# adaLN columns queued behind given units of weights, and gates written out and read back some units apart

## The chip, the cores and the metric

The kernel runs on one core of one Trainium2 chip. The metric is device time in microseconds (us) of one execution; lower is better. The engines are TensorE (PE, matmuls; PEld is its weight load), VectorE (DVE), ScalarE (ACT), GpSimd (POOL) and SyncE (SP), which here issues nearly all DMA transfers in one in-order queue (SPq).

## The reference

Two layers of a transformer-like backbone on 256 latent and 256 context tokens, model width 1024. Layer 0 mixes tokens by bidirectional retention (4 heads), layer 1 by neighbourhood attention (16 heads); each mixer is followed by a SwiGLU with hidden width 2816. Everything is modulated (adaLN): from the conditioning vectors `c` (latent) and `c_ctx` (context) come six rows per layer, a shift, a scale and a gate for each of the two sub-layers. Cut to what matters:

```
cond_lat = silu(c)[:, None, :]; cond_ctx = silu(c_ctx)[None, None, :]
for i in range(2):
    want_ctx = i < 1
    m_lat = split(cond_lat @ ada_w[i] + ada_b[i], 6)      # shift, scale, gate, shift, scale, gate
    m_ctx = split(cond_ctx @ ada_w[i] + ada_b[i], 6)
    a_lat = h_lat * (1 + m_lat[1]) + m_lat[0]             # and a_ctx alike
    y_ctx, y_lat = retention_mixer(...) if i == 0 else neighbourhood_mixer(...)
    h_lat = layer_norm(ALPHA * h_lat + m_lat[2] * y_lat, ln_g[i, 0], ln_b[i, 0])
    f_lat = swiglu(h_lat * (1 + m_lat[4]) + m_lat[3], ffn_w13[i], ffn_w2[i])
    h_lat = layer_norm(ALPHA * h_lat + m_lat[5] * f_lat, ln_g[i, 1], ln_b[i, 1])
    # the same for h_ctx while want_ctx
return h_lat
```

## The kernel before

**Matmuls and the stream of weights.** A matmul in fp32 is made of three in fp32r (`mm3`, L139 to L143): each operand is split into a high part (the value rounded to fp32r) and a low part (the rest), and the products high·high, low·high and high·low are summed in PSUM. All weight matrices pass once through SBUF as 228 "units" of 128 x 1024 fp32 (512 KB). The class `Stream` (L83 to L135) does that in three steps: `load_to` issues the load of `raw{u}` on SP (L110, three buffers); `split_to` has ACT cast the high part `whi{u}` (L123) and DVE subtract to get the low part `wlo{u}` (L125; a few on POOL), five buffers each; `next()` hands a unit to the matmuls after it has split units ahead (`ahead` = 4) and issued loads three further. Most units feed 24 matmuls of 512 columns.

**The order of the work.** Most of the program is ordered by a scheduler that simulates the engines' timelines and may issue a ready instruction earlier than where the code stands; some stretches are ordered as written (`manual_schedule`). Within an engine, and in SP's queue, instructions run in the order they are issued, each waiting for its own semaphores, so one that waits holds up all behind it.

**The adaLN columns.** The class `Ada` (L193 to L248) computes `silu(c) @ ada_w + ada_b` not on PE but on DVE: one "job" is 128 output columns, whose weights are loaded as `adaraw{i}` (128 x 1024 fp32, 512 KB, L218, two buffers), and one DVE instruction `junk{i}_{s}` (L226) multiplies them by the broadcast condition and sums along the row into one column of `ada{l}{s}`; s = 0 is latent, s = 1 context. There are 96 jobs. Jobs 0 to 15 (layer 0, shift and scale of the mixer) run at the start. Then come for layer 0 the mixer's gate (16 to 23), scale (24 to 31) and shift (32 to 39) of the SwiGLU, and its gate (40 to 47); for layer 1 scale and shift of the mixer (48 to 63), then, latent only and so one instruction each, its gate (64 to 71), scale (72 to 79), shift (80 to 87) and gate of the SwiGLU (88 to 95). `pump()` is called once per unit handed out and runs jobs by a credit per unit (`RATES`, 0.5, 0.7 or 1.0 by the number of jobs done), but the scheduler may move the instructions forward. `hooks` are functions called when a given number of jobs is done.

**Gates.** A gate is needed as a row on all partitions. `load_gate` (L266) stores the eight gate columns to DRAM (`gscr`, 128 x 8, 4 KB, L269) and reads the row back broadcast to 128 partitions as `gateb` (512 KB, L271). The two DMAs are issued one after the other on SP, and the second waits for the first to land. The gates of layer 0 are made by a hook at 24 jobs (mixer) and inside the first SwiGLU (`mix0`, `gate_hook`, at its fourth hidden block); those of layer 1 inside the attention (j = 2) and in the last SwiGLU. `make_affine` (L707) combines layer norm weights with scale and shift in three tiny POOL operations.

**Where they are used.** The retention's output projection `out_half` gives four PSUM tiles `w` of 512 columns; `head_add` (L591) has DVE multiply each by the gate into `t2` (two buffers) and POOL (or DVE) add it to `z`. In the SwiGLU, `hidden` makes the tiles `f` and DVE multiplies them with the SiLU part into `hf` (L813); `d` is the second matmul. `qf1k` (L457 on DVE, L462 its cast) is the rotary evacuation of the keys of head 1.

Of the kernel before, what the change touches and what calls it, by code (L numbers as in the profile page):

```python
# [8 lines left out]
F32 = mybir.dt.float32  # L9
# [3 lines left out]
ALU = mybir.AluOpType  # L13
# [5 lines left out]
P = 128  # L19
D = 1024  # L20
# [24 lines left out]
def backbone(ctx: ExitStack, tc: tile.TileContext, wpack, adapack, cond, condcol, xT, xtok, adab, lncol, lnrow,  # L45
             decay, delta, rope, rpb, mask8, out):
    nc = tc.nc
# [8 lines left out]
    act = ctx.enter_context(tc.tile_pool(name="act", **HIGH))  # L56
# [26 lines left out]
    class Stream:  # L83
# [21 lines left out]
        def load_to(self, n):  # L105
            n = min(n, self.total)
            while self.loaded < n:
                i = self.loaded
                t = wst.tile([P, UNIT], F32, tag="raw", name=f"raw{i}", bufs=3)
                nc.sync.dma_start(t, wpack[i])  # L110
                self.raw[i] = t
                self.loaded += 1

        def split_to(self, n):
            n = min(n, self.total)
            while self.split < n:
                u = self.split
                self.load_to(u + 1)
                raw = self.raw.pop(u)
                pool, th, tl, bufs = self.place.get(u, (wsplit, "whi", "wlo", self.BUFS))  # L120
                hi = pool.tile([P, UNIT], F32R, tag=th, name=f"whi{u}", bufs=bufs)
                lo = pool.tile([P, UNIT], F32R, tag=tl, name=f"wlo{u}", bufs=bufs)
                nc.scalar.copy(hi, raw)  # L123
                eng = nc.gpsimd if u in self.on_pool else nc.vector
                eng.tensor_tensor(out=lo, in0=raw, in1=hi.bitcast(F32), op=ALU.subtract)  # L125
                self.units[u] = (hi, lo)
                self.split += 1

        def next(self):
            self.split_to(self.used + self.ahead)  # L130
            self.load_to(self.split + 3)
            u = self.used
            self.used += 1
            ada.pump()
            return self.units.pop(u)  # L135

    stream = Stream()
# [17 lines left out]
    l0 = l0stack.enter_context(tc.tile_pool(name="l0", **HIGH))  # L155
# [37 lines left out]
    class Ada:  # L193
# [43 lines left out]
                    self.hooks.pop(self.done)()  # L237


        RATES = ((48, 0.5), (64, 0.7), (96, 1.0))  # L240

        def pump(self):
            if self.done < 16:
                return
            self.credit += next((r for n, r in self.RATES if self.done < n), 1.0)
            while self.credit >= 1:
                self.credit -= 1
                self.run(self.done + 1)  # L248

    ada = Ada()  # L250

# [11 lines left out]
    gscr = dram.tile([2, 2, 2, D], F32, name="gscr")  # L263
    gateb = {}

    def load_gate(l, g, s):  # L266

        scr = gscr[l, g, s]
        nc.sync.dma_start(scr.rearrange("(k p) -> p k", p=P), adacol[l][s][:, 8 * (3 * g + 2):8 * (3 * g + 2) + 8])  # L269
        t = (act, l0)[s].tile([P, D], F32, tag=f"gate{s}", name=f"gateb{l}{g}{s}")  # L270
        nc.sync.dma_start(t, scr.unsqueeze(0).partition_broadcast(P))  # L271
        gateb[(l, g, s)] = t

    lnrows = {}

# [28 lines left out]
    with Phase("ret", "yTh", "yTl", "vh", "vl", "kh", "kl") as rp:  # L304
# [466 lines left out]
        for t in CTX_FIRST:  # L771
            for half in range(2):
# [1 line left out]
                xr = rp.tile([P, 512], F32, tag="pf", name=f"xr{t}{half}", bufs=2)  # L774
                nc.sync.dma_start(xr, xtok[t, :, cs])
                nc.gpsimd.tensor_scalar(out=z[t][:, cs], in0=xr, scalar1=ALPHA, scalar2=0.0, op0=ALU.mult, op1=ALU.add)
        ada.hooks[24] = lambda: [load_gate(0, 0, s) for s in range(2)]
        ada.hooks[40] = lambda: [make_affine(0, 0, 0, 1, s) for s in range(2)]
        for h in range(RET_H):
            scores(h)  # L780
# [19 lines left out]
    with Phase("ffn", "hh", "hl") as fp:  # L800
# [23 lines left out]
        def mix0(part):  # L824

            js = list(range(HF))
            if part == 0:
                u0 = units(2)
                hidden(0, 0, u0, 256, 256, hcols(0, 256, 256))
                Feed(fam_of(fp), 0, 0, (0, 1)).all()  # L830
                u1 = units(2)
                hidden(0, 1, u1, 256, 256, hcols(1, 256, 256))
                region.__exit__(None, None, None)
                hidden(0, 0, u0, 0, 256, hcols(0, 0, 256))
                hidden(0, 1, u1, 0, 256, hcols(1, 0, 256))
                load_ln(fp, ("ln0", "ln1", "ln2", "ln3"), 0, 0)
                for t in CTX_FIRST:
                    residual(0, 0, t)
                js = js[2:]
            for j in js:  # L840
                hidden(0, HF * part + j, units(2), 0, 512, hid[j])
                if (part, j) == (0, 3):
                    for s in range(2):
                        gate_hook(0, 1, s)

            cur = {}

            def piece(half, k):
                n = half * HF + k
                if n // 2 not in cur:  # L850
                    cur[n // 2] = stream.next()
                return cut(cur[n // 2], slice(None), slice((n % 2) * 512, (n % 2) * 512 + 512))

            for half in range(2):
                cs = slice(half * 512, half * 512 + 512)
                ps = {t: bank(f"d{part}_{half}_{t}") for t in CTX_FIRST}
                tail = 7 if (part, half) == (1, 1) else 1
                groups = [[k] for k in range(HF - tail)] + [list(range(HF - tail, HF))]
                for grp in groups:
                    ms = [piece(half, k) for k in grp]  # L860

                    def products(t, n0=0, n1=len(grp)):
                        for k, m in list(zip(grp, ms))[n0:n1]:
                            mm3(ps[t], cut(hid[k], slice(None), slice(t * P, t * P + P)), m, k == 0, k == HF - 1)

                    if (part, half) == (1, 1) and grp[-1] == HF - 1:
                        return last_rows(products, ps)
                    for t in CTX_FIRST:
                        products(t)
                        if grp[-1] == HF - 1:  # L870
                            gate_add(0, 1, t, cs, ps[t], nc.vector if part else nc.gpsimd)
# [33 lines left out]
            normalise(1, *mr)  # L905
            return region

        def gate_hook(l, g, s):
            load_gate(l, g, s)

        mix0(0)
        ada.run(64)
        for s in range(2):
            make_affine(0, 1, 1, 0, s)
        T3, E3, E4, BB, FB, E5 = 2, 2, 7, range(7), 4, 2
        region = mix0(1)
        ada.run(96)
    l0stack.close()


    with Phase("na", "oTh", "oTl", "qs") as ap:
# [164 lines left out]
        for j in range(KT - 2):  # L1086
            load_bias(j + 2)
            kq(j + 2)
            na_transposes(j)
            if j == KT - 3:  # L1090
                region.__exit__(None, None, None)
                region = tc.manual_schedule(engines={PE, DVE, POOL, ACT})
                region.__enter__()
            na_scores(j + 1)
            na_products(j)
            if j < KT - 3:
                make_bias(j + 2)
            if j == 2:
                load_gate(1, 0, 0)
                make_affine(1, 0, 1, 1, 0)  # L1100


# [56 lines left out]
    with Phase("ffn1", "h1h", "h1l") as fp:  # L1159
# [51 lines left out]
                if RX:  # L1211
                    region.__exit__(None, None, None)

        load_gate(1, 1, 0)
        load_ln(fp, ("ln0", "ln1", "ln2", "ln3"), 1, 0)
        with tc.issue_after(last_pool.ins):
            for t in range(2):
# [154 lines left out]
```

## Time and profile before

| | us |
|---|---|
| median of 3 timed runs (lowest, highest) | 1241.11 (1240.41, 1245.79) |
| the profiled execution | 1235.01 |
| its span | 1233.2 |
| DVE, low parts `wlo` L125, 217 instructions | 287.2 busy |
| DVE, columns `junk` L226, 160 instructions | 215.0 busy, 81.1 idle just before them |
| landing of a unit's load `raw`, median | 4.1 |
| mean TensorE clock granted, of full speed | 0.981 |

A profile row of instructions names the source line, the engine, the operation and the tiles as output<-inputs, with the numbers in the names left out. In rows of waits the waiting line comes first, then the instruction that released it, then microseconds in total, number of times and the longest. A timeline row has start, duration, instruction and, in brackets, how long the engine had been idle before it and what ended that.

### The profile page before, as it was taken

Reading aid. Unit: us, or ns where it says so; the run is one execution under the profiler, and the core shown is the slowest. Engines: PE = TensorE matmul, PEld = TensorE weight load, DVE = VectorE, ACT = ScalarE, POOL = GpSimd, SP = SyncE. Lnnn points to the kernel's source line nnn. Section 1 sums busy time; section 2 is a strip of 40 time slices with the busy share of each in tenths; the row PEclk is TensorE's granted clock in tenths of the full one; section 3 lists DMA queues with packets and bytes.
Section 4 is the critical chain, followed back from the end, with each engine's and each line's share of the span. In section 5 each row is a group of like instructions: output and inputs, shape, how many; then the busy total and the mean of one; then the engine's idle time right before and its main releaser. Section 6 shows DMA issues by size and latency. Waiting matters only on the chain.

```text
span 1233.2 us, 15925 instructions
## 1 busy us (share of the span) xinstructions
PE 1172.8 (95%) x5990; PEld 985.8 (80%) x5990; DVE 769.5 (62%) x1079; ACT 441.0 (36%) x670; POOL 316.4 (26%) x304
## 2 busy tenths in 40 slices
PE   7989898999999999899879999999999998999996
PEld 5668686888888888688668788887888876999985
DVE  7898599833543589399567633247455576766544
ACT  3553231422333243122111333215354464555430
POOL 1521114412211568000002200006535446300003
PEclk9989999999999999999979999999999999999998
DMA  9855666523223223567988523324478744777550
GB/s 357 304 196 144 160 215 197 164 78 94 99 69 103 70 95 95 108 232 241 204 273 267 153 90 103 97 74 141 137 210 216 232 133 132 233 220 230 183 160 35
DMA packets 70156, 201.76 MB, mean 164 GB/s; under 512 B 14528, under 2 KB 17344, under 8 KB 70080
## 3 DMA queue, kind: packets, MB, share of 16 engines
q1 hardware_dynamic: 69648, 200.10, 53.4%
q8 instruction: 47, 0.77, 0.3%
q10 hardware_dynamic: 432, 0.66, 0.1%
q14 instruction: 29, 0.24, 0.1%
HBM read 187.98 MB, written 2.25 MB: 154 GB/s over the span
## 4 chain that ended last, share of the span: by engine, by line
PE 45%; DMA 7%; DVE 6%; issue 2%; POOL 1%; ACT 0%; SPq 0%; POOLq 0%; DVEq 0%; ACTq 0%
PE f L143 6%; PE f L142 6%; PE f L141 6%; DMA adaraw<-in_adapack 5%; PE d L142 2%; PE d L143 2%; PE d L141 2%; DVE junk L226 2%; DMA gscr<-ada 2%; PE e L141 2%; PE e L142 2%; PE e L143 2%; PE o L1058 1%; PE k L141 1%; DVE wlo L125 1%
## 5 line engine op out<-in xcount | busy, mean ns | idle before, releaser
L125 DVE TENSOR_TENSOR wlo<-raw,whi 128x1024 fp32r<-128x1024 f32 x217 | 287.2, 1329 | 226.2 <-ACT whi L123 219.5
L123 ACT CAST whi<-raw 128x1024 fp32r<-128x1024 f32 x220 | 229.4, 1048 | 427.4 <-DMA raw<-in_wpack 166.1
L226 DVE CUSTOM_DVE_ANT_0 junk<-adaraw,cond,adab_sb 128x1024 bf16<-128x1024 f32 x160 | 215.0, 1344 | 81.1 <-DMA adaraw<-in_adapack 79.1
L143 PE MATMUL f<-aTh,wlo 128*128 128x256 f32 (+1 forms) x704 | 233.9, 333 | 6.4 <-DVE wlo L125 6.2
L142 PE MATMUL f<-aTl,whi 128*128 128x256 f32 (+1 forms) x704 | 234.0, 333 | 3.4 <-DVE aTl L727 3.3
L141 PE MATMUL f<-aTh,whi 128*128 128x256 f32 (+1 forms) x704 | 233.3, 332 | 0.0
L143 PEld LDWEIGHTS f<-aTh,wlo 128*128 128x128 f32 x704 | 133.8, 190 | 20.3 <-DVE wlo L125 7.6
L142 PEld LDWEIGHTS f<-aTl,whi 128*128 128x128 f32 x704 | 133.8, 190 | 17.1 <-DVE aTl L727 4.1
L141 PEld LDWEIGHTS f<-aTh,whi 128*128 128x128 f32 x704 | 133.6, 190 | 12.6
L299 POOL TENSOR_SCALAR pa_n<-bmv 128x1 f32<-128x1 f32 x12 | 3.2, 269 | 319.1 <-DVE bmv L677 318.9
L142 PE MATMUL d<-wlo,hh 128*128 128x512 f32 x176 | 69.8, 397 | 11.6 <-DVE wlo L125 11.6
L141 PE MATMUL v<-whi,aTh 128*128 128x512 f32 x168 | 66.7, 397 | 4.8 <-ACT qf1k L462 4.8
L143 PE MATMUL d<-whi,hl 128*128 128x512 f32 x176 | 69.6, 395 | 0.0
L141 PE MATMUL d<-whi,hh 128*128 128x512 f32 x176 | 69.5, 395 | 0.0
L143 PE MATMUL v<-whi,aTl 128*128 128x512 f32 x168 | 66.2, 395 | 1.9 <-POOL aTl L727 1.9
L142 PE MATMUL v<-wlo,aTh 128*128 128x512 f32 x168 | 66.2, 394 | 0.0
L593 POOL TENSOR_TENSOR z<-t,z 128x512 f32<-128x512 f32 x28 | 46.4, 1667 | 71.6 <-DVE t L591 71.6
L141 PE MATMUL g<-aTh,whi 128*128 128x512 f32 x128 | 50.2, 392 | 1.8 <-ACT qf0q L462 1.8
L150 ACT CAST hh<-hf 128x512 fp32r<-128x512 f32 (+1 forms) x24 | 14.0, 585 | 102.4 <-DVE hf L813 102.4
L141 PE MATMUL w<-whi,yTh 128*128 128x512 f32 x128 | 49.9, 391 | 0.0
L142 PE MATMUL g<-aTl,whi 128*128 128x512 f32 x128 | 49.8, 389 | 0.0
L143 PE MATMUL g<-aTh,wlo 128*128 128x512 f32 x128 | 49.8, 389 | 0.0
(277 smaller groups left out, 2271.3 us busy)
## 6 DMA issues: line engine op xcount, KB each, us to landing
raw<-in_wpack SPq DMA_DIRECT2D x228, 512.0 KB, 4.1
adaraw<-in_adapack SPq DMA_DIRECT2D x96, 512.0 KB, 4.3
ln<-in_lnrow SPq DMA_DIRECT2D x16, 256.0 KB, 4.3
braw<-in_rpb SPq DMA_DIRECT2D x8, 512.0 KB, 5.2
kh<-sth SPq DMA_DIRECT2D x32, 128.0 KB, 2.3
kl<-stl SPq DMA_DIRECT2D x32, 128.0 KB, 2.4
gateb<-gscr SPq DMA_DIRECT2D x6, 512.0 KB, 5.0
xt<-in_xT SPq DMA_DIRECT2D x8, 256.0 KB, 6.1
```

The lines of the kernel that those rows point to most:

```text
L123: nc.scalar.copy(hi, raw)
L125: eng.tensor_tensor(out=lo, in0=raw, in1=hi.bitcast(F32), op=ALU.subtract)
L141: nc.tensor.matmul(o, s[0], m[0], start=start, stop=False)
L142: nc.tensor.matmul(o, s[0], m[1], start=False, stop=False)
L143: nc.tensor.matmul(o, s[1], m[0], start=False, stop=stop)
L150: return (nc.scalar.copy(pair[0], src), (lo_eng or nc.vector).tensor_tensor(out=pair[1], in0=src, in1=pair[0].bitcast(F32), op=ALU.subtract))
L226: nc.vector.tensor_tensor_reduce(out=junk, in0=self.tiles[i], in1=condb[s], scale=1.0, scalar=adab_sb[:, l, m:m + 1], op0=ALU.mult, op1=AL ...
L299: nc.gpsimd.tensor_scalar(out=a, in0=src, scalar1=scale, scalar2=eps, op0=ALU.mult, op1=ALU.add)
L593: eng.tensor_tensor(out=z[t][:, cs], in0=t2, in1=z[t][:, cs], op=ALU.add)
L1058: nc.tensor.matmul(b[hh * 64:hh * 64 + 64, :NLAT], vf[kk][:, c:c + 64], pts[(hh, kk // 2)][:, kk % 2, :], start=kk == 0, stop=kk == 3)
```

## The change

`pump` now takes the unit u that is about to be split and gives credits by u (`RATES` by unit). Each column instruction is queued on DVE behind the latest `wlo` made there (`tc.issue_after(stream.last_low.ins)`), so that the scheduler cannot move it ahead of that. The loads `adaraw` are queued on SP behind the last load of a unit (`prefetch`). `load_gate` is cut in two, `store_gate` and `load_gate`, each queued behind the last load of a unit: for the mixer of layer 0 at 25 and 27 jobs, for its SwiGLU at 49 and 52, for the attention at 74 jobs and in the attention at j = 2, for the last SwiGLU before the attention and in that SwiGLU. `gate_hook` and `ada.run(64)` are gone, and the affine factors of layer 1 hang on a hook at 64 jobs. Line numbers in the changed kernel are higher: `raw` L110, `wlo` L126, `adaraw` L221, `junk` L229, the gate's store L280, its read-back L288, `t2` L608, `hf` L831.

```diff
@@ split_to
                 u = self.split
                 self.load_to(u + 1)
+                ada.pump(u)
                 raw = self.raw.pop(u)
...
-                eng.tensor_tensor(out=lo, in0=raw, in1=hi.bitcast(F32), op=ALU.subtract)
+                low = eng.tensor_tensor(out=lo, in0=raw, in1=hi.bitcast(F32), op=ALU.subtract)
+                if u not in self.on_pool:
+                    self.last_low = low
@@ next
             self.load_to(self.split + 3)
+            ada.prefetch()
             u = self.used
             self.used += 1
-            ada.pump()
@@ class Ada
-        RATES = ((48, 0.5), (64, 0.7), (96, 1.0))
-
-        def pump(self):
-            if self.done < 16:
-                return
-            self.credit += next((r for n, r in self.RATES if self.done < n), 1.0)
-            while self.credit >= 1:
+        RATES = ((11, 0.0), (20, 1.0), (62, 0.42), (70, 0.0), (86, 0.55), (104, 0.9), (127, 1.3))
+
+        def pump(self, u):
+
+            self.credit += next((r for n, r in self.RATES if u < n), 0.0)
+            while self.credit >= 1 and self.done < len(self.jobs):
                 self.credit -= 1
-                self.run(self.done + 1)
+                with tc.issue_after(stream.last_low.ins):
+                    self.run(self.done + 1)
+
+        def prefetch(self):
+
+            if self.loaded < self.done + 2:
+                with tc.issue_after(stream.last_load.ins):
+                    self.load_to(self.done + 2)
@@ gates
-    def load_gate(l, g, s):
-
-        scr = gscr[l, g, s]
-        nc.sync.dma_start(scr.rearrange("(k p) -> p k", p=P), adacol[l][s][:, 8 * (3 * g + 2):8 * (3 * g + 2) + 8])
-        t = (act, l0)[s].tile([P, D], F32, tag=f"gate{s}", name=f"gateb{l}{g}{s}")
-        nc.sync.dma_start(t, scr.unsqueeze(0).partition_broadcast(P))
-        gateb[(l, g, s)] = t
+    def store_gate(l, g, streams):
+
+        with tc.issue_after(stream.last_load.ins):
+            for s in streams:
+                nc.sync.dma_start(gscr[l, g, s].rearrange("(k p) -> p k", p=P),
+                                  adacol[l][s][:, 8 * (3 * g + 2):8 * (3 * g + 2) + 8])
+
+    def load_gate(l, g, streams):
+
+        with tc.issue_after(stream.last_load.ins):
+            for s in streams:
+                t = (act, l0)[s].tile([P, D], F32, tag=f"gate{s}", name=f"gateb{l}{g}{s}")
+                nc.sync.dma_start(t, gscr[l, g, s].unsqueeze(0).partition_broadcast(P))
+                gateb[(l, g, s)] = t
@@ retention
-        ada.hooks[24] = lambda: [load_gate(0, 0, s) for s in range(2)]
+        ada.hooks[25] = lambda: store_gate(0, 0, (0, 1))
+        ada.hooks[27] = lambda: load_gate(0, 0, (0, 1))
         ada.hooks[40] = lambda: [make_affine(0, 0, 0, 1, s) for s in range(2)]
@@ first SwiGLU
-                if (part, j) == (0, 3):
-                    for s in range(2):
-                        gate_hook(0, 1, s)
...
+        ada.hooks[49] = lambda: store_gate(0, 1, (0, 1))
+        ada.hooks[52] = lambda: load_gate(0, 1, (0, 1))
+        ada.hooks[74] = lambda: store_gate(1, 0, (0,))
+        ada.hooks[64] = lambda: [make_affine(0, 1, 1, 0, s) for s in range(2)]
         mix0(0)
-        ada.run(64)
-        for s in range(2):
-            make_affine(0, 1, 1, 0, s)
...
         region = mix0(1)
         ada.run(96)
+        store_gate(1, 1, (0,))
```

What moves shows in the order of instructions on the engines. First place: SP's queue at the first gate, in the retention of head 1. A row is line, operation, output<-inputs and size; `gscr` is the store, `gateb` the read-back. Before:

```order
L420 DMA Dt1_830<-dscr_131 128x768
L269 DMA gscr_100<-ada00_84 128x8x1
L110 DMA raw20_919<-in_wpack 128x1024
L271 DMA gateb000_1362<-gscr_100 128x1024
L269 DMA gscr_100<-ada01_85 128x8x1
L218 DMA adaraw25_1488<-in_adapack 128x1024
L271 DMA gateb001_1365<-gscr_100 128x1024
L110 DMA raw21_950<-in_wpack 128x1024
```

And now:

```order
L280 DMA gscr_100<-ada00_84 128x8x1
L221 DMA adaraw25_984<-in_adapack 128x1024
L280 DMA gscr_100<-ada01_85 128x8x1
L110 DMA raw22_1123<-in_wpack 128x1024
L221 DMA adaraw26_1125<-in_adapack 128x1024
L110 DMA raw23_1155<-in_wpack 128x1024
L110 DMA raw24_1185<-in_wpack 128x1024
L110 DMA raw25_1219<-in_wpack 128x1024
L221 DMA adaraw27_1221<-in_adapack 128x1024
L110 DMA raw26_1278<-in_wpack 128x1024
L288 DMA gateb000_1311<-gscr_100 128x1024
L288 DMA gateb001_1313<-gscr_100 128x1024
```

The stores now stand behind raw21 instead of ahead of raw20 and raw21, and five loads of units and three of columns, raw22 to raw26 and `adaraw25` to `adaraw27`, stand ahead of the read-backs.

Second place: DVE at the output projection of retention head 0, whose evacuations are `t2_...`. Before:

```order
L591 SCALAR_TENSOR_TENSOR t2_020_1425<-w0_0_2_1412,pb_r0_1241,gateb001_1365 128x512
L226 ISA junk39_0_2911,ada00_84<-adaraw39_2909,cond0_78,adab_sb_80 128x1024
L226 ISA ada00_84 128x1
L591 SCALAR_TENSOR_TENSOR t2_030_1441<-w0_0_3_1428,pb_r0_1241,gateb001_1365 128x512
L226 ISA junk39_1_2913,ada01_85<-adaraw39_2909,cond1_79,adab_sb_80 128x1024
L226 ISA ada01_85 128x1
L226 ISA junk40_0_3008,ada00_84<-adaraw40_3006,cond0_78,adab_sb_80 128x1024
L226 ISA ada00_84 128x1
L591 SCALAR_TENSOR_TENSOR t2_000_1457<-w0_0_0_1444,pb_r0_1241,gateb000_1362 128x512
L226 ISA junk40_1_3010,ada01_85<-adaraw40_3006,cond1_79,adab_sb_80 128x1024
L226 ISA ada01_85 128x1
L125 TENSOR_TENSOR wlo29_1477<-raw29_1353,whi29_1476 128x1024
```

And now:

```order
L608 SCALAR_TENSOR_TENSOR t2_020_1447<-w0_0_2_1434,pb_r0_1271,gateb001_1313 128x512
L229 ISA junk28_1_1500,ada01_85<-adaraw28_1321,cond1_79,adab_sb_80 128x1024
L229 ISA ada01_85 128x1
L608 SCALAR_TENSOR_TENSOR t2_030_1463<-w0_0_3_1450,pb_r0_1271,gateb001_1313 128x512
L608 SCALAR_TENSOR_TENSOR t2_000_1479<-w0_0_0_1466,pb_r0_1271,gateb000_1311 128x512
L126 TENSOR_TENSOR wlo29_1503<-raw29_1387,whi29_1502 128x1024
L608 SCALAR_TENSOR_TENSOR t2_010_1495<-w0_0_1_1482,pb_r0_1271,gateb000_1311 128x512
```

Between the first three evacuations stood three column instructions and a fourth before `wlo29`; now there is one. Job 28 is done here, where before it was job 40: the jobs in between run later.

Third place: DVE in the SwiGLU of layer 0 around the job 74, whose predecessors complete the attention's gate. Before:

```order
L125 TENSOR_TENSOR wlo90_4610<-raw90_4499,whi90_4609 128x1024
L226 ISA junk73_0_5235,ada10_86<-adaraw73_5233,cond0_78,adab_sb_80 128x1024
L226 ISA ada10_86 128x1
L151 TENSOR_TENSOR hl10_3543<-hf0_10_0_4564,hh10_3542 128x512
L226 ISA junk74_0_5301,ada10_86<-adaraw74_5299,cond0_78,adab_sb_80 128x1024
L226 ISA ada10_86 128x1
L226 ISA junk75_0_5311,ada10_86<-adaraw75_5309,cond0_78,adab_sb_80 128x1024
L226 ISA ada10_86 128x1
L125 TENSOR_TENSOR wlo91_4646<-raw91_4511,whi91_4645 128x1024
```

And now:

```order
L229 ISA junk73_0_5291,ada10_86<-adaraw73_5231,cond0_78,adab_sb_80 128x1024
L229 ISA ada10_86 128x1
L831 TENSOR_TENSOR hf0_14_0_5284<-f0_14_1_0_5234,sg0_14_0_5283 128x512
L126 TENSOR_TENSOR wlo109_5307<-raw109_5219,whi109_5306 128x1024
L229 ISA junk74_0_5304,ada10_86<-adaraw74_5300,cond0_78,adab_sb_80 128x1024
L229 ISA ada10_86 128x1
L154 TENSOR_TENSOR hl3_3521<-hf0_14_0_5284,hh3_3520 128x512
L229 ISA junk75_0_5370,ada10_86<-adaraw75_5302,cond0_78,adab_sb_80 128x1024
L229 ISA ada10_86 128x1
L126 TENSOR_TENSOR wlo110_5373<-raw110_5229,whi110_5372 128x1024
```

The same jobs now stand 19 units later, behind unit 109 instead of 90, with one low part more between job 73 and job 75.

More of the change, by code (lines that the diff above doesn't have):

```diff
@@ L109, in load_to @@
                 t = wst.tile([P, UNIT], F32, tag="raw", name=f"raw{i}", bufs=3)
-                nc.sync.dma_start(t, wpack[i])
+                self.last_load = nc.sync.dma_start(t, wpack[i])
                 self.raw[i] = t
@@ L906, in last_rows @@
             return region
-        def gate_hook(l, g, s):
-            load_gate(l, g, s)
+        ada.hooks[49] = lambda: store_gate(0, 1, (0, 1))
+        ada.hooks[52] = lambda: load_gate(0, 1, (0, 1))
+        ada.hooks[74] = lambda: store_gate(1, 0, (0,))
+        ada.hooks[64] = lambda: [make_affine(0, 1, 1, 0, s) for s in range(2)]
         mix0(0)
-        ada.run(64)
-        for s in range(2):
-            make_affine(0, 1, 1, 0, s)
         T3, E3, E4, BB, FB, E5 = 2, 2, 7, range(7), 4, 2
@@ L1098, in backbone @@
             if j == 2:
-                load_gate(1, 0, 0)
+                load_gate(1, 0, (0,))
                 make_affine(1, 0, 1, 1, 0)
@@ L1212, in backbone @@
                     region.__exit__(None, None, None)
-        load_gate(1, 1, 0)
+        load_gate(1, 1, (0,))
         load_ln(fp, ("ln0", "ln1", "ln2", "ln3"), 1, 0)
```

## The prediction

> **What bounds the kernel now.** I read the page first, then the list of what TensorE waited for, then the timeline at each long wait.
>
> ```profile
> PE 1172.8 (95%) x5990; PEld 985.8 (80%) x5990; DVE 769.5 (62%) x1079; ACT 441.0 (36%) x670; POOL 316.4 (26%) x304
> ```
>
> TensorE (PE) is busy for 1172.8 of 1233.2 us, so the time is its own work plus its stalls, 1233.2 − 1172.8 = 60.4 us of idle time, plus what it runs at a lower clock behind a stall. VectorE (DVE), at 62%, matters only where PE waits for it. The second view says where (waiting line, releaser, us in all, times, longest).
>
> ```profile
> PE d L142 <- DVE wlo L125: 11.6, 1, 11.6
> PE f L143 <- DVE wlo L125: 6.2, 2, 4.9
> PE v L141 <- ACT qf1k L462: 4.8, 1, 4.8
> PE f L142 <- DVE aTl L727: 3.3, 4, 1.4
> ```
>
> These are few and long waits, single accidents and not a steady shortage. In the timelines below a row is start, duration, instruction and, in brackets, the idle time before it with its releaser. First the 4.8 us wait, A:
>
> ```profile
> 131.27 0.39 PE L142 MATMUL v<-wlo,aTh 128*128 128x512 f32 x1
> ...
> 132.86 0.39 PE L143 MATMUL v<-whi,aTl 128*128 128x512 f32 x1
> 138.03 0.80 PE L141 MATMUL v<-whi,aTh 128*128 128x512 f32 x1 [4.78 <-ACT qf1k L462]
> ...
> 141.54 0.39 PE L143 MATMUL v<-whi,aTl 128*128 128x512 f32 x1
> ```
>
> From 131.27 to 132.86 seven matmuls start: 1.59 / 7 = 0.227 us from start to start, while a row says 0.39 (they overlap). So a gap costs its bracket and 0.39 − 0.227 = 0.16 us more. Behind the gap eight matmuls take 141.54 − 138.03 = 3.51 us instead of 8 × 0.227 = 1.82: another 1.69 us. A costs 4.78 + 0.16 + 1.69 = 6.6 us.
>
> What caused it stands on SyncE's DMA queue (SPq) and on DVE:
>
> ```profile
> 111.51 0.38 SPq L269 DMA_DIRECT2D gscr<-ada  x1
> 113.18 0.34 SPq L110 DMA_DIRECT2D raw<-in_wpack  x1
> 121.45 0.32 SPq L271 DMA_DIRECT2D gateb<-gscr  x1
> 121.86 0.39 SPq L269 DMA_DIRECT2D gscr<-ada  x1
> 122.30 0.57 SPq L218 DMA_DIRECT2D adaraw<-in_adapack  x1
> 133.79 0.32 SPq L271 DMA_DIRECT2D gateb<-gscr  x1
> ```
>
> ```profile
> 134.39 1.28 DVE L226 CUSTOM_DVE_ANT_0 junk<-adaraw,cond,adab_sb 128x1024 bf16<-128x1024 f32 x1 [14.01 <-DMA adaraw<-in_adapack]
> 135.60 0.08 DVE L226 DVE_READ_ACCUMULATOR2_ANT ada<- 128x1 f32 x1
> 135.60 1.22 DVE L125 TENSOR_TENSOR wlo<-raw,whi 128x1024 fp32r<-128x1024 f32 x1
> 136.74 0.42 DVE L457 SCALAR_TENSOR_TENSOR qf1k<-k,cosT 128x256 f32<-128x256 f32 x1
> ```
>
> The 4 KB gate store is slow: its read-back is issued 9.9 us after the first store and 11.9 us after the second, and nothing else is issued on SPq meanwhile. The column's weights (`adaraw`), issued 0.44 us behind the second store, land only when DVE starts at 134.39, 12.1 us later, so a load behind a store also waits. DVE stood 14 us at that column, and the low part `wlo` and the evacuation of `k`, which PE needed, stood behind it.
>
> B is another kind:
>
> ```profile
> 208.48 0.39 PE L141 MATMUL S<-qh,kh 128*128 128x256 f32 x1 [1.57 <-DVE t L591]
> ...
> 212.53 0.80 PE L141 MATMUL q<-aTh,whi 128*128 128x512 f32 x1 [3.08 <-DVE t L591]
> ...
> 216.54 0.40 PE L141 MATMUL q<-aTh,whi 128*128 128x512 f32 x1
> ```
>
> ```profile
> 200.00:220.00 20.00, 15.35 (x65) 12.37 (x64) 19.22 (x22) 2.10 (x2) 14.95 (x9) 0.83 0.48 146
> ```
>
> The window row gives length, then busy time of PE, weight load, DVE, ACT, POOL: DVE is full (19.22 of 20 us) with columns laid between the evacuations `t` of the output projection. B costs 1.57 + 3.08 + 2 × 0.16, and behind the second gap nine matmuls in 4.01 instead of 2.04: 1.97. Sum 6.9 us.
>
> C and D are A's kind, with a `wlo` right behind the waiting column:
>
> ```profile
> 522.01 0.80 PE L143 MATMUL f<-aTh,wlo 128*128 128x512 f32 x1 [4.89 <-DVE wlo L125]
> ...
> 527.23 0.40 PE L143 MATMUL f<-aTh,wlo 128*128 128x512 f32 x1
> ```
>
> ```profile
> 519.52 1.28 DVE L226 CUSTOM_DVE_ANT_0 junk<-adaraw,cond,adab_sb 128x1024 bf16<-128x1024 f32 x1 [19.06 <-DMA adaraw<-in_adapack]
> ```
>
> ```profile
> 623.58 0.79 PE L142 MATMUL d<-wlo,hh 128*128 128x512 f32 x1 [11.62 <-DVE wlo L125]
> ...
> 629.64 0.39 PE L141 MATMUL d<-whi,hh 128*128 128x512 f32 x1
> ```
>
> ```profile
> 602.73 0.43 SPq L269 DMA_DIRECT2D gscr<-ada  x1
> 604.23 0.33 SPq L218 DMA_DIRECT2D adaraw<-in_adapack  x1
> ```
>
> ```profile
> 617.79 1.28 DVE L226 CUSTOM_DVE_ANT_0 junk<-adaraw,cond,adab_sb 128x1024 bf16<-128x1024 f32 x1 [6.91 <-DMA adaraw<-in_adapack]
> ```
>
> C: 4.89 + 0.16 + (5.22 − 12 × 0.227 = 2.50) = 7.6 us. D: 11.62 + 0.16 + (6.06 − 14 × 0.227 = 2.88) = 14.7 us; here a load issued 1.5 us behind a store landed 13.6 us later. E is the second, shorter wait of `f` L143, 6.2 − 4.9 = 1.3, so 1.5 us with its 0.16, and it came just behind a store:
>
> ```profile
> 679.07 0.38 SPq L269 DMA_DIRECT2D gscr<-ada  x1
> ```
>
> F, at the start, is a wait for `aTl`, with a column and a `wlo` ahead of it on DVE:
>
> ```profile
> 64.22 0.80 PE L142 MATMUL qk<-aTl,whi 128*128 128x512 f32 x1 [3.89 <-DVE aTl L330]
> ...
> 69.86 0.39 PE L143 MATMUL v<-whi,aTl 128*128 128x512 f32 x1
> ```
>
> **The change, part by part.** No instruction is added or removed on any engine, only moved.
>
> Gate stores and read-backs (A, C, D, E). The wait that goes is this one, on SPq:
>
> ```profile
> SPq L271 <- DMA gscr<-ada: 41.5, 4, 11.8
> ```
>
> Weights are now issued between store and read-back, as the order shows for the first gate. But the stores still hold up what is behind them in the DMA queue, 12.1 us each by A, 24.2 for a pair. What covers that: a unit keeps PE for 24 × 0.227 = 5.45 us, and four units are split ahead of it, 21.8 us, with up to three more loaded.
>
> ```profile
> DMA to landing us min/median/max: 3.4/4.3/13.4
> ```
>
> ```profile
> L141 PE MATMUL g<-aTh,whi x32: 389/389/478, 159.6 to 180.8; 128*128 128x512 f32 x32
> ```
>
> The first row is the landing of the columns' loads, 512 KB as those of the units. First pair: `g` of the next head begins at 159.6 with unit 20, so unit 22 was needed at 170.5 and without A's 6.6 us at 164. The stores are issued near 122; raw22 behind them lands near 122 + 24.2 + 4.3 = 150.5, and `wlo22` is there at 153: 11 us to spare. Second pair: raw83 is issued when `wlo80` frees its buffer, eight units (43.6 us) before PE needs unit 84, and 43.6 − 24.2 − 4.3 − 2.5 (a column and a split) leaves 13. Third, a single store: raw111 and two `adaraw` queue behind it and `wlo110` stands behind both columns, 12.1 + 4.3 + some 5 + 2.5 = 24, while PE needs unit 110 about 30 us after `wlo108`: 6 to spare. If that cover is gone, the stall is as before. I take the whole of A, C, D and E: 6.6 + 7.6 + 14.7 + 1.5 = 30.4 us. It cannot be more; the other end is what the first rival gives.
>
> Columns pinned behind given units (B, D). At B one column instruction stands between the four evacuations where there were four; the others move to later units, as those of D do. What do they meet there?
>
> ```profile
> L226 DVE CUSTOM_DVE_ANT_0 junk<-adaraw,cond,adab_sb x160: 1267/1284/2310, 6.8 to 677.8; 128x1024 bf16<-128x1024 f32 x160
> ```
>
> ```profile
> 630.00:680.00 50.00, 50.00 (x223) 41.39 (x222) 37.09 (x50) 9.41 (x10) 10.13 (x5) 1.00 0.82 266
> 690.00:760.00 70.00, 70.00 (x310) 57.99 (x309) 28.28 (x31) 25.21 (x32) 0.00 (x0) 1.00 0.43 134
> ```
>
> A column instruction takes 1.28 us (minimum, median and maximum in ns above). The new rates reach 1.3 columns per unit in units 104 to 126, which fall mostly behind 690: 28.28 / 70 × 5.45 = 2.2 us of DVE per unit, plus 1.3 × 1.28 = 1.7, makes 3.9 of 5.45. The traffic would be 2.3 × 524 KB in 5.45 us = 221 GB/s, and 266 GB/s passed in 630 to 680 with PE busy throughout. So columns there cost nothing; without that cover each would cost PE 1.28. B's 6.9 us goes, all or, if POOL's additions to `z` are next late (14.95 of 20 us above), none; I take all, since POOL has 5 us free there.
>
> The Trainium skill, "SBUF — State Buffer", section "Who interferes with whom", says that a DVE instruction with two SBUF inputs contends with a GpSimd instruction that reads SBUF. That speaks against columns in retention heads, where POOL adds to `z`; the trace agrees, the longest column above being 2.31 us against 1.27. By it some 24 column instructions at 1.0 us more are 24 us of DVE spread over the 220 us from 230 to 450, an estimate; the sum is unchanged.
>
> Start (F). The first column goes behind the `aTl` work, taking 1.27 us from a gap of 3.89. Upper end: the slow run behind the gap (5.64 − 13 × 0.227 = 2.7) also vanishes and a second moved column gives as much again, 1.27 + 2.7 + 1.27 = 5.2; lower end 0, as `wlo` alone may set it. I take 1.3, as the new gap, 2.6, is nearer to the 3.08 of B, which went slow, than to 1.57, which did not.
>
> First FFN. Matmuls of the first two hidden blocks are interleaved otherwise. Of the `aTl` L727 waits (3.3 us) between all and none may go, or as much be added; I take 0.
>
> Affine factors on POOL move a little; they are some tiny operations, and POOL is not waited for there. Sum: 30.4 + 6.9 + 1.3 = 38.6 us. The profiled execution took 1235.01 us, 1.8 more than its span, and would take 1196.4. The timed median is 6.1 above it, so 1241.1 − 38.6 = **1202.5**, say 1203.
>
> **The rivals.**
> 1. The stores still clog. The pairs hold up 24 us of loads; if only two split units are left there instead of four, A's and C's `wlo` are late again, 6.6 + 7.6 us: 1217. For it: D's load waited 13.6 us though SPq itself did not. Against: nothing PE needs soon stands behind the stores. The Trainium skill, "DMA: Bandwidth & Descriptors", section "Queues, rings and completion order", has descriptors consumed in ring order on each DMA engine, which is this rival's ground; the trace agrees (12.1 us at 122.30).
> 2. Slower. Each pinned column has only two `adaraw` buffers, and a `wlo` stands behind it on DVE. Two loads take a landing plus 1.6 us. At 1.3 columns per unit PE starves once (landing + 1.6) / 2 × 1.3 exceeds 5.45, from 6.8 us on. At the maximum of the landings, 13.4, a unit takes 9.75: 4.3 lost × 23 units = 99, less 21.8 of cover, 77; minus the gain, 1241 + 77 − 39 = 1279. The median of 4.3 speaks against it.
> 3. It does nothing: other waits take the place of the old ones at the same places, each as long. About 1239. The moved rows in the order speak against it.
> 4. The clock. After gaps of 3.08 us and more PE ran slow, after 1.57 it did not; if a 2.6 us gap at F stays fast, 2.7 more is gained: 1200. The Trainium skill, "TensorE: Matmul & The Clock Gate", section "What's actually happening", puts the drop after an idle window of about 3.4 us. By that rule F stays fast; the trace agrees for 3.89 and differs at 3.08, which had 1.57 just ahead.
>
> **How the numbers follow.** Forecast 1203: 0.60. Rival 4: 0.13. Rival 1: 0.14. Rival 3: 0.05. Rival 2: 0.08. Low end: 1202.5 − (5.2 − 1.3) − 3.3 = 1195.3, rounded to 1196. High end: 1217 and the first FFN's 3.3, rounded to 1221. That leaves out rivals 2 and 3, 13%. A measurement can tell about 0.5%, 6 us. Faster 0.87, within 0.5% 0.05, slower 0.08.
>
> **What would show it.** In the new profile PE's idle time falls from 60 to about 33 us; the waits of `d` and `f` for `wlo` and of `v` for `qf1k` are gone; SPq's wait of 41.5 us at the read-back falls to a few; DVE never stands over 10 us at a column with a `wlo` PE needs behind it; `t` at the first output projection no longer holds PE. Wrong would be: a `wlo` wait of PE after raw21, raw83 or raw110 (rival 1), a row of short ones in units 104 to 126 (rival 2).

## The result, and the profile after

| us | before | after |
|---|---|---|
| median of 4 runs each | 1243.45 | 1194.95 |
| lowest, highest | 1240.41, 1247.38 | 1194.14, 1197.83 |
| ratio, 95% interval | | 0.9621 (0.9596 to 0.9646) |
| the profiled execution, its span | 1235.01, 1233.2 | 1197.83, 1196.0 |

The medians are 48.5 us apart, the profiled executions 37.2. The forecast was a gain of 38.6 and 1203 us; the measured median is 1 us below the low end of the range (worked out as 1195.3, but put at 1196). First the page of the changed kernel and its list of what PE waited for, all rows of 1.8 us and more:

```profile
PE 1164.8 (97%) x5990; PEld 982.9 (82%) x5990; DVE 769.2 (64%) x1079; ACT 443.2 (37%) x670; POOL 306.9 (26%) x304
```

```profile
PE cond L182 <- DVE chi L175: 5.1, 1, 5.1
PE f L145 <- DVE aTl L744: 4.0, 3, 1.4
PE hr L146 <- DVE aTl L744: 2.4, 3, 1.6
PE qk L145 <- DVE aTl L347: 1.9, 1, 1.9
PE v L146 <- POOL aTl L744: 1.8, 3, 0.9
PE hr L146 <- POOL aTl L744: 1.8, 1, 1.8
```

PE's idle time is 1196.0 − 1164.8 = 31.2 us, where it was 60.4. No wait for `wlo`, `qf1k` or `t` is left; busy time fell too, by 8.0 us at the same number of matmuls, as fewer ran slow behind a gap (mean granted clock 0.990, before 0.981).

Where the 37.2 us came from is read from landmarks: the first and last start of a group of matmuls in both traces ("count: shortest, median, longest duration in ns, first to last start"). Before:

```profile
L141 PE MATMUL g<-aTh,whi x24: 389/389/497, 74.1 to 89.8; 128*128 128x512 f32 x24
...
L141 PE MATMUL q<-aTh,whi x16: 389/389/796, 212.5 to 224.7; 128*128 128x512 f32 x16
...
L565 PE MATMUL ss<-ones,sqsum x32: 169/250/250, 158.8 to 424.9; 128*128 128x1 f32 x32
...
L141 PE MATMUL d<-whi,hh x88: 388/389/628, 584.4 to 658.2; 128*128 128x512 f32 x88
...
L141 PE MATMUL v<-whi,aTh x64: 389/389/481, 841.8 to 889.5; 128*128 128x512 f32 x64
```

And after:

```profile
L144 PE MATMUL g<-aTh,whi x28: 389/390/497, 71.0 to 89.5; 128*128 128x512 f32 x28
...
L144 PE MATMUL g<-aTh,whi x32: 389/389/478, 149.9 to 171.1; 128*128 128x512 f32 x32
...
L144 PE MATMUL q<-aTh,whi x16: 389/390/398, 197.8 to 208.0; 128*128 128x512 f32 x16
...
L582 PE MATMUL ss<-ones,sqsum x32: 169/250/251, 149.1 to 408.1; 128*128 128x1 f32 x32
...
L144 PE MATMUL d<-whi,hh x88: 388/389/390, 562.7 to 621.8; 128*128 128x512 f32 x88
...
L144 PE MATMUL v<-whi,aTh x64: 389/389/628, 803.8 to 853.1; 128*128 128x512 f32 x64
```

The lead of the changed kernel is the difference of two such starts (the second `g`, 159.6 before, stands in the prediction). It grows in steps:

| up to | lead | step | predicted |
|---|---|---|---|
| first `g` (F) | 74.1 − 71.0 = 3.1 | 3.1 | 1.3 |
| second `g` (A) | 159.6 − 149.9 = 9.7 | 6.6 | 6.6 |
| last `q` of head 2 (B) | 224.7 − 208.0 = 16.7 | 7.0 | 6.9 |
| last `ss`, retention's end | 424.9 − 408.1 = 16.8 | 0.1 | 0 |
| first `d` (first SwiGLU begins; C) | 584.4 − 562.7 = 21.7 | 4.9 | 7.6 |
| last `d` of the first half (D) | 658.2 − 621.8 = 36.4 | 14.7 | 14.7 |
| first `v` of layer 1 (E) | 841.8 − 803.8 = 38.0 | 1.6 | 1.5 |
| end of the span | 1233.2 − 1196.0 = 37.2 | −0.8 | 0 |

### The profile page after: what moved, and what is told of

Same layout as the page of the kernel before. It is cut to its first block, busy times and chain, and to the rows that moved or that the text cites. A ratio compares the mean times of both kernels' runs of the same rounds, so it can differ in the third digit from the quotient of the medians.

```text
span 1196.0 us, 15876 instructions
## 1 busy us (share of the span) xinstructions
PE 1164.8 (97%) x5990; PEld 982.9 (82%) x5990; DVE 769.2 (64%) x1079; ACT 443.2 (37%) x670; POOL 306.9 (26%) x304
## 4 chain that ended last, share of the span: by engine, by line
PE 88%; DVE 4%; DMA 3%; POOL 2%; ACT 2%; issue 1%; SPq 0%; POOLq 0%; DVEq 0%; ACTq 0%
PE f L145 10%; PE f L146 10%; PE f L144 10%; PE d L145 3%; PE d L146 3%; PE d L144 3%; PE v L146 3%; PE v L144 3%; PE v L145 3%; PE g L144 2%; PE g L146 2%; PE g L145 2%; PE w L144 2%; PE w L146 2%; PE w L145 2%; PE k L144 2%
## 5 line engine op out<-in xcount | busy, mean ns | idle before, releaser
L126 DVE TENSOR_TENSOR wlo<-raw,whi 128x1024 fp32r<-128x1024 f32 x217 | 279.2, 1291 | 230.9 <-ACT whi L124 222.4
L229 DVE CUSTOM_DVE_ANT_0 junk<-adaraw,cond,adab_sb 128x1024 bf16<-128x1024 f32 x160 | 221.1, 1382 | 31.3 <-DMA adaraw<-in_adapack 28.8
L610 POOL TENSOR_TENSOR z<-t,z 128x512 f32<-128x512 f32 x28 | 43.3, 1558 | 75.0 <-DVE t L608 75.0
L145 PE MATMUL w<-wlo,yTh 128*128 128x512 f32 x128 | 49.8, 390 | 0.0
```

The source lines that it names most:

```text
L126: low = eng.tensor_tensor(out=lo, in0=raw, in1=hi.bitcast(F32), op=ALU.subtract)
L145: nc.tensor.matmul(o, s[0], m[1], start=False, stop=False)
L229: nc.vector.tensor_tensor_reduce(out=junk, in0=self.tiles[i], in1=condb[s], scale=1.0, scalar=adab_sb[:, l, m:m + 1], op0=ALU.mult, op1=AL ...
L610: eng.tensor_tensor(out=z[t][:, cs], in0=t2, in1=z[t][:, cs], op=ALU.add)
```

## The experiments

All stand beside runs of the kernel before on the same chip; a ratio is to those. Before had a median of 1241.64 us (13 runs), 1240.05 and 1241.91 (7 runs each) in the three sets. "The changed kernel" is at 0.9621.

**Is the profiled execution a typical one?** The kernel before, unchanged, once more.

> The kernel before, unchanged, profiled a second time. If the profiled execution of before is a typical one, this one has the same span within 2 us and the same stalls A to D (6.6, 6.9, 7.6, 14.7 us). If the stalls vary from run to run, as the timed runs of before do (1240.41 to 1247.38), its span is some 1238 to 1246 and the surplus stands in longer gaps at the same four places, with a lower granted clock than the kernel after.

Ten runs went from 1236.74 to 1248.2, median 1240.97, ratio 0.9999 (0.9973 to 1.0025). Its own profiled execution has a span of 1236.8 us, 3.6 more than the first one's:

```profile
PE d L142 <- DVE wlo L125: 12.6, 2, 11.4
PE f L143 <- DVE wlo L125: 7.8, 3, 4.8
PE v L141 <- ACT qf1k L462: 5.4, 1, 5.4
```

The sites are the same, but there is a second wait of `d` and a third of `f`, and the one of `v` is 0.6 longer. The stalls differ between the two executions, and the execution behind the prediction was shorter than any of the 23 timed runs of this set (from 1235.27 up).

**The read-backs alone.** Before, with only the read-back moved behind a unit's load; the stores stay where they were, and on DVE each column stands at most one low part later than before.

```diff
-        nc.sync.dma_start(t, scr.unsqueeze(0).partition_broadcast(P))
+        with tc.issue_after(stream.last_load.ins):
+            nc.sync.dma_start(t, scr.unsqueeze(0).partition_broadcast(P))
```

> The kernel before with one edit: the read-back of a gate is queued on SP behind the last load of a unit, so SP never waits for a store to land; the order on DVE stays that of before, row for row. By the prediction's split (stores and read-backs carry A and C, 6.6 + 7.6 us) it gains 14 us: ratio about 0.989. By the rival, that the store holds up the column's load in the DMA queue and DVE's order then holds up PE, A and C stay: within 4 us of before, ratio 0.997 to 1.003, and DVE still stands over 10 us at a column near 134 and near 519.

1226.62 us, ratio 0.9885 (0.9837 to 0.9932): the 14 us that the expectation gives to A and C, but only in part from these places.

```profile
PE d L142 <- DVE wlo L125: 8.2, 1, 8.2
...
PE v L141 <- ACT qf1k L463: 4.5, 1, 4.5
...
PE q L141 <- DVE t L592: 3.1, 1, 3.1
```

C is gone and D is 3.4 us shorter, but A is there as before (`v`, 4.5). On DVE, the column ahead of `wlo19` still waits, for a load that queues behind the two stores:

```profile
135.44 1.28 DVE L226 CUSTOM_DVE_ANT_0 junk<-adaraw,cond,adab_sb 128x1024 bf16<-128x1024 f32 x1 [14.78 <-DMA adaraw<-in_adapack]
```

So at A it was not SP's wait that held PE, but the order on DVE together with the store in the DMA queue.

**The columns alone.** The changed kernel with store, read-back, store, read-back in a row for both gates of layer 0, `prev` being the last DMA queued:

```diff
-        with tc.issue_after(stream.last_load.ins):
-            for s in streams:
+        prev = stream.last_load
+        for s in streams:
+            with tc.issue_after(prev.ins):
+                prev = nc.sync.dma_start(gscr[l, g, s]..., adacol[l][s]...)
...
+            with tc.issue_after(prev.ins):
+                prev = nc.sync.dma_start(t, gscr[l, g, s].unsqueeze(0).partition_broadcast(P))
```

> The changed kernel with the two pairs of gates of layer 0 made as before: store, read-back, store, read-back, one right behind the other on SP, so that SP waits for both stores; the columns stay pinned as in the change. By the prediction's split A and C come back: 14 us above the changed kernel, about 1209. By the rival (the order on DVE alone) nothing comes back: within 3 us of the changed kernel, 1192 to 1198, and SP waits some 45 us at the read-backs without PE noticing.

1195.5 us, ratio 0.963 (0.9579 to 0.9682): nothing comes back, although SP waits as long as before:

```profile
SPq L300 <- DMA gscr<-ada: 42.4, 4, 12.1
```

With the columns spread, the split of the gates of layer 0 is worth nothing that can be measured; in the kernel before, its read-backs alone are worth 14 us. They are not two gains to be added. (Layer 1's gates stay here as the change has them.)

**Density.** The columns as close together as before had them, but pinned, with split gates (the two read-backs hang on later job numbers, so that they stand some units behind their stores):

```diff
-        RATES = ((11, 0.0), (20, 1.0), (62, 0.42), (70, 0.0), (86, 0.55), (104, 0.9), (127, 1.3))
+        RATES = ((11, 0.0), (31, 1.4), (68, 0.0), (101, 1.65))
```

> The changed kernel, with the columns packed as densely as before had them (1.4 jobs per unit in units 11 to 30, 1.65 in units 68 to 100, still pinned each behind its low part), gates split as in the change. If B's and D's stalls come from the density of the columns, they return: B 6.9 and a part of D's 14.7, 1202 to 1217. If pinning and split gates are what counts, it stays within 3 us of the changed kernel, 1192 to 1198.

1227.26 us, ratio 0.9883 (0.9835 to 0.9932): above its expectation, 32 us of the gain are gone. The long waits have become many short ones:

```profile
PE f L146 <- DVE wlo L126: 7.1, 6, 2.7
PE d L145 <- DVE wlo L126: 6.1, 4, 2.3
...
PE S L144 <- DVE t L608: 5.0, 2, 3.1
```

Then the two places apart, with `RATES` of `dense` in units 11 to 30 alone and from unit 68 on alone:

```diff
+        RATES = ((11, 0.0), (31, 1.4), (70, 0.0), (86, 0.45), (104, 0.9), (127, 1.3))          # dense_ret
+        RATES = ((11, 0.0), (20, 1.0), (62, 0.42), (68, 0.0), (101, 1.65))                      # dense_ffn
```

> The changed kernel with the columns of units 11 to 30 packed as in dense (1.4 jobs per unit), the rest spread as in the change. If what dense lost is the sum of two places, this one shows the first: at the second head's q, dense stood 10 us behind the changed kernel, so 1203 to 1207, with waits of PE for t at the first output projection. If density costs only together with the dense columns of the SwiGLU, it stays at 1192 to 1198.

> The changed kernel with the columns of the first SwiGLU packed as in dense (1.65 jobs per unit in units 68 to 100), the rest spread as in the change. By the sum of two places it loses the other 18 to 21 us: 1211 to 1217, in short waits of f and d for wlo. If the density does not matter in the SwiGLU, where PE's 5.45 us per unit leave DVE more room, 1192 to 1198.

1204.93 us (0.9693, 0.9664 to 0.9721) and 1209.59 us (0.974, 0.9713 to 0.9767). Against 1195 that is 10 us for the retention, B's place, as expected, and 14.6 for the SwiGLU, a little less than expected; the sum, 24.6, is 7.7 short of `dense`, and where the rest arises stays open. In the second one, D's stall is back at a store, although SP waits for nothing there:

```profile
604.58 0.79 PE L145 MATMUL d<-wlo,hh 128*128 128x512 f32 x1 [7.28 <-DVE wlo L126]
```

**What is dense: DVE or the loads?** `dense` with columns that read a quarter of their weights; loads as they were. The modulation is then that of a quarter of the sum.

```diff
-                out=junk, in0=self.tiles[i], in1=condb[s], scale=1.0, ...
+                out=junk[:, :256], in0=self.tiles[i][:, :256], in1=condb[s][:, :256], scale=1.0, ...
```

> The kernel dense with one edit: each column instruction multiplies and sums 256 of the 1024 weights of a row, so it takes about 0.4 us instead of 1.28; loads are unchanged (the modulation is that of a quarter of the sum). If the dense columns cost because DVE's own time runs out, the time falls to 1192 to 1205. If they cost because the columns' loads (two buffers, landing 4.3 us and more, behind the units' loads) come late, it stays above 1215 and DVE goes on waiting some 60 us for adaraw.

1203.41 us, ratio 0.9703 (0.9685 to 0.9722): 22 to 24 of the 32 us return (by the ratios and by the medians), so DVE's own time is most of what density costs. A column takes 0.485 us, and DVE now waits more for the loads, not less, which costs PE one stall each at D's and A's places:

```profile
L229 DVE CUSTOM_DVE_ANT_0 junk<-adaraw,cond,adab_sb x160: 466/485/1520, 7.2 to 637.8; 128x256 bf16<-128x256 f32 x160
its engine sat idle before it (us, times) until:
  DMA adaraw<-in_adapack: 148.1, 78
```

```profile
PE d L145 <- DVE wlo L126: 6.8, 1, 6.8
...
PE v L144 <- ACT qf1k L482: 3.9, 1, 3.9
```

**Pins.** The changed kernel without the pin on DVE, and then without that on the loads either:

```diff
-                with tc.issue_after(stream.last_low.ins):
-                    self.run(self.done + 1)
+                self.run(self.done + 1)
@@ and for rates_free also
-                with tc.issue_after(stream.last_load.ins):
-                    self.load_to(self.done + 2)
+                self.load_to(self.done + 2)
```

> The changed kernel without the pin of column instructions behind a low part on DVE; their loads stay queued behind the units' loads on SP, so the order keeps nearly the same density (job 40 behind unit 54 instead of 57, job 64 behind 99 instead of 100). If the spreading over units is what brings the gain: within 3 us of the changed kernel, 1192 to 1198. If the exact place behind the low part matters: 4 us or more above it, with waits of PE for t, wlo or qf1k.

> The changed kernel with neither pin: rates by unit and split gates as in the change, but columns and their loads free for the scheduler. It moves them forward again to where before had them (job 40 behind unit 28, job 92 behind 101). If the density is what costs, the time goes back to that of gates_only or dense, 1222 to 1232, with waits of PE for t and wlo. If the rates or the call at the split do it, it stays near 1195.

1195.47 us (0.9652, 0.9623 to 0.9681): the pin on DVE is not needed while the loads are pinned, since a column cannot run ahead of its load. And 1213.45 us (0.979, 0.9766 to 0.9814): without either the scheduler moves the columns forward again and 18 us are lost, the density's waits among them:

```profile
PE S L144 <- DVE t L606: 4.1, 2, 3.1
PE d L145 <- DVE wlo L126: 3.8, 4, 1.8
```

That is less than 1222, the low end of what was expected; with the gates split and the stores pinned, A's and D's long stalls do not come back, though the columns are as close as before: in the retention each stands behind the same number of low parts as in the kernel before, in the SwiGLU all but the first two jobs at most five later. So `rates_free` is also the nearest thing to the gates alone, stores and read-backs: 1240.05 − 1213.45 = 26.6 us better than before. DVE waits at A's place here too, but behind the evacuations of `k` and not ahead of them:

```profile
125.58 0.41 DVE L472 SCALAR_TENSOR_TENSOR rm_1k<-k,sinT 128x256 f32<-128x256 f32 x1
135.23 1.28 DVE L229 CUSTOM_DVE_ANT_0 junk<-adaraw,cond,adab_sb 128x1024 bf16<-128x1024 f32 x1 [9.24 <-DMA adaraw<-in_adapack]
```

And the store of D's place comes when no column is left behind it (the last one started at 672.0):

```profile
683.92 0.43 SPq L278 DMA_DIRECT2D gscr<-ada  x1
```

`dense`, whose columns are as close, took 14 us more; whether that is its pins or its stores, with columns right behind them, was not tried.

**The cover.** The changed kernel with each store issued twice, the first to a scratch that nobody reads:

```diff
+                for n in range(EXTRA):
+                    nc.sync.dma_start(gscr2[n, l, g, s].rearrange("(k p) -> p k", p=P),
+                                      adacol[l][s][:, 8 * (3 * g + 2):8 * (3 * g + 2) + 8])
                 nc.sync.dma_start(gscr[l, g, s].rearrange("(k p) -> p k", p=P),
```

> The changed kernel with each gate's store issued twice in a row (the first into a scratch that nobody reads), so a pair of gates holds up the queue for some 24 us more and a single gate for 12 us more. By the prediction's count of cover (11, 13 and 6 us to spare) PE waits some 12, 10 and 6 us at the low parts behind them, with the slow matmuls behind each gap some 35 us: about 1230. If the cover is larger, because the stores overlap or the stream has more ahead, the time stays within 6 us of the changed kernel, 1193 to 1201.

1197.23 us, ratio 0.9668 (0.9637 to 0.9699): no stall. These are the first store, the unit queued behind all four, and ACT getting that unit:

```profile
114.68 0.43 SPq L283 DMA_DIRECT2D gscr<-ada  x1
...
119.38 19.51 SPq L110 DMA_DIRECT2D raw<-in_wpack  x1
```

```profile
154.21 1.05 ACT L124 CAST whi<-raw 128x1024 fp32r<-128x1024 f32 x1 [19.86 <-DMA raw<-in_wpack]
```

The queue is held, as predicted: 154.2 − 114.7 = 39.5 us for four stores, a column's load and a unit, so at most (39.5 − 4.1) / 4 = 8.9 a store. The count of cover went wrong in two numbers: a store takes 9 us in such a row, not 12 (A's 12.1 us hold the landing of the load behind the store, which the count adds once more), and the first is issued at 114.7, not near 122. The split of the unit is done near 156.5, and PE needs it, two units of 5.45 us behind the start of `g`, here at 150.2, at 161.1.

**A higher rate, and a longer pause.** The second rival's place, and an attempt at the start of the first SwiGLU:

```diff
+        RATES = ((11, 0.0), (20, 1.0), (62, 0.42), (70, 0.0), (86, 0.55), (95, 0.9), (127, 2.0))    # rate2
+        RATES = ((11, 0.0), (20, 1.0), (57, 0.42), (70, 0.0), (86, 0.65), (104, 0.9), (127, 1.3))   # pause57
```

> The changed kernel with 2.0 jobs per unit from unit 95 on instead of 0.9 and 1.3; all of these jobs are latent only, so one column instruction each. DVE then needs 1.2 + 2 x 1.28 + 0.65 = 4.4 of 5.45 us per unit, so if DVE's time is the limit it holds: 1192 to 1199. By the second rival of the prediction (two buffers, starving once landing + 1.6 us for two columns exceeds a unit, 5.45, so from a landing of 3.9 us on) DVE waits for adaraw in every unit and the store behind job 73 finds less cover: 1203 or more.

> The changed kernel with the pause of the columns before the first SwiGLU begun at unit 57 instead of 62 (0.65 instead of 0.55 per unit behind it), so that no column stands on DVE while the SwiGLU starts, where POOL is busy and a column takes 2.3 us. If those columns cause the 2.7 us that the changed kernel loses there against before, 1190 to 1194. If the order of matmuls does, no change: 1193 to 1198.

1195.66 us (0.9618, 0.9591 to 0.9644) and 1196.61 us (0.9638, 0.9608 to 0.9667): neither differs from the changed kernel. Two columns per unit hold in units 95 and up, where each is one instruction. No version tried beats the change.

## Why the prediction was right, and where not

**The bound.** Right: PE's few long waits and the slow matmuls behind them were the time to be had. The steps at A, B, D and E came within 0.1 us of their terms.

**Which part carries the gain.** Wrong. The prediction gave A, C, D and E, 30.4 us, to the gates and only B and F, 8.2 us, to the columns, as terms to be added. The runs show that they overlap. The spread columns alone give all of the gain (`columns_only`), and both together no more. The read-backs alone give 14 us (`gates_only`), stores and read-backs some 27 with the columns close together (`rates_free`): the long waits of A, C and D are gone there, and B's is left (`q` for `t`, 2.4 us). A needs three things: a store in the DMA queue, a column's load behind it, and that column on DVE ahead of work that PE waits for. In `rates_free` the third is missing, and spreading takes it away too. In the changed kernel the column behind the first store comes after `wlo`, with no evacuation behind it, and finds its load landed:

```profile
134.06 1.23 DVE L126 TENSOR_TENSOR wlo<-raw,whi 128x1024 fp32r<-128x1024 f32 x1 [0.89 <-ACT whi L124]
135.20 1.28 DVE L229 CUSTOM_DVE_ANT_0 junk<-adaraw,cond,adab_sb 128x1024 bf16<-128x1024 f32 x1
```

At D's store a column still waits, and PE is busy throughout (window: PE 80.00 of 80 us), because the units ahead of it are split:

```profile
676.43 1.28 DVE L229 CUSTOM_DVE_ANT_0 junk<-adaraw,cond,adab_sb 128x1024 bf16<-128x1024 f32 x1 [8.10 <-DMA adaraw<-in_adapack]
```

```profile
600.00:680.00 80.00, 80.00 (x355) 66.27 (x354) 48.07 (x61) 20.57 (x24) 8.86 (x7) 1.00 0.58 188
```

Dense columns had used up that lead before the store came (`dense_ffn`: 7.28 us at the same job). So D, too, goes with the density, though not with that alone: in `rates_free`, where the columns are dense but the store comes behind them all, it is gone as well.

**C, and the first SwiGLU.** C's 7.6 us are gone, since no wait for `wlo` is left, but in this execution 2.7 of them were given back at the SwiGLU's start, taken at 0 with a bound of 3.3. Behind a gap of 1.38 us some 27 matmuls of 256 columns ran slow:

```profile
453.24 0.58 PE L145 MATMUL f<-aTl,whi 128*128 128x256 f32 x1 [1.38 <-DVE aTl L744]
...
459.10 0.30 PE L145 MATMUL f<-aTl,whi 128*128 128x256 f32 x1
459.24 0.28 PE L146 MATMUL f<-aTh,wlo 128*128 128x256 f32 x1
```

From 453.24 to 459.24 that is 6.0 us for what takes 27 × 0.12 = 3.2 at the full clock: 2.8 us. It is no fixed price of the change. From the last `ss` to the first `d` pass 159.5 us in the kernel before and 154.6 in this execution, but 150.2 in `columns_only`, and 150.3 in `store_twice`, `rate2` and `pause57`, where the waits for `aTl` are shorter (the longest after the first 0.5) and nothing runs slow; there the step is 9.2 or 9.3, C's 7.6 and 1.6 or 1.7 more. `columns_only`:

```profile
L595 PE MATMUL ss<-ones,sqsum x32: 169/250/250, 149.8 to 408.8; 128*128 128x1 f32 x32
L144 PE MATMUL d<-whi,hh x88: 389/389/389, 559.0 to 618.2; 128*128 128x512 f32 x88
```

So the columns at the SwiGLU's start, which `pause57` took away, are not its cause: `rate2`, which is the changed kernel up to unit 95, has them and lacks the loss too. What decides stays open.

**F.** 3.1 instead of 1.3, within its bounds of 0 and 5.2: the gap went from 3.89 to 1.90 us, by 2.0 and not by one column, and the slow matmuls behind it cost 1.5 us instead of 2.7.

**The size on the clock.** The sum was made against the profiled execution, and there it holds: 38.6 predicted, 37.2 found. The step that failed is the last one, which carried the 6.1 us between that execution and the median over to the new kernel. The 6.1 us were taken to be fixed, but they did not stay. `before_again` shows 3.6 of them as longer and added stalls, mostly at the same places; that the rest is of this kind too is likely and not shown. The median gained 6.1 + 2.3 more at that end (1243.45 now, not 1241.1), and the new kernel's profiled execution was its slowest run, 1197.83 against a median of 1194.95: 37.2 + 8.4 + 2.9 = 48.5. Against 1202.5 the median is 7.5 lower: 6.1 + 2.9 − 1.4.

**The rivals.** Stores that clog: the queue is held, by 9 to 12 us a store, but the cover is larger than counted, and even twice the stores cost nothing. The Trainium skill, "DMA: Bandwidth & Descriptors", section "Queues, rings and completion order", has descriptors consumed in ring order on each DMA engine; the 39.5 us of `store_twice` agree. Columns that starve: did not happen, and not at 2.0 per unit either (`rate2`). A change that does nothing: `rates_free` shows how it could have, the scheduler undoing 18 us of it. The clock: the start stayed slow behind 1.90 us, so the price was not gained there. The Trainium skill, "TensorE: Matmul & The Clock Gate", section "What's actually happening", has the clock drop after an idle window of some 3.4 us; the runs differ, as the last section shows.

## What to carry to other kernels

Side work on an engine that also feeds the bound engine costs nothing while it is spread thinly enough that the feeding work stays ahead; packed densely, it eats the lead, and then a late transfer stalls the bound engine. Before adding up what two parts of a change remove, ask whether one stall needs both causes: removing either may remove it all. And where the runs of a kernel spread, the profile of one run prices the stalls of that run: other runs have more of them, and a change that removes the stalls can gain more than that profile shows.

## What was not expected of the hardware

The clock of PE does not drop by the length of a gap alone. Rows behind gaps, where 0.63 us in the next row is slow and 0.39 to 0.40 is full speed. The changed kernel:

```profile
62.92 0.60 PE L145 MATMUL qk<-aTl,whi 128*128 128x512 f32 x1 [1.90 <-DVE aTl L347]
63.32 0.63 PE L146 MATMUL qk<-aTh,wlo 128*128 128x512 f32 x1
...
810.59 0.72 PE L146 MATMUL v<-whi,aTl 128*128 128x512 f32 x1 [0.86 <-POOL aTl L744]
811.11 0.63 PE L144 MATMUL v<-whi,aTh 128*128 128x512 f32 x1
```

The kernel before, at the same place as the last:

```profile
848.56 0.50 PE L143 MATMUL v<-whi,aTl 128*128 128x512 f32 x1 [0.86 <-POOL aTl L727]
848.90 0.40 PE L141 MATMUL v<-whi,aTh 128*128 128x512 f32 x1
```

The kernel before, profiled again:

```profile
686.36 0.50 PE L143 MATMUL f<-aTh,wlo 128*128 128x512 f32 x1 [2.57 <-DVE wlo L125]
686.69 0.40 PE L141 MATMUL f<-aTh,whi 128*128 128x512 f32 x1
```

The same gap of 0.86 us (with 0.74 and 0.24 shortly before it) was followed by slow matmuls in one execution and not in the other, and behind the one of 2.57 us nothing ran slow. Such stretches of slow matmuls, 1.5 to 2.8 us each, are a part of why executions of one kernel differ. What decides was not tried.
